# A decoder block's down projection as seven block products in eight parts, with three weight sums formed in DRAM

## Chip, cores, metric

One core of a Trainium2 chip runs the whole program. The metric is the device time of one execution in microseconds. Three runs of the kernel before gave 2439.49, 2440.13 and 2441.36 us; their median is 2440.13. A change of under 0.2% (4.9 us) is treated as no change.

## The reference, cut to what matters

`x` has 512 tokens of 2048 channels; everything is float32.

```python
def _sq_relu_mlp(h, w_up, w_down):
    return jnp.square(jax.nn.relu(h @ w_up)) @ w_down

h = x
for l in range(DEPTH):                       # DEPTH = 1
    a = _rmsnorm(h, norm1_w[l])
    h = h + _token_mix(a, w_in[l], ...)      # four head groups and an output projection
    m = _rmsnorm(h, norm2_w[l])
    h = h + _sq_relu_mlp(m, w_ffn_up[l], w_ffn_down[l])
return _rmsnorm(h, final_norm_w)
```

The change concerns the last product: the hidden activations, 512 x 8192, times `w_ffn_down`, 8192 x 2048, added to `h`, and the final norm. What is computed stays the same up to rounding.

## The kernel before, in words

**Float32 products as three matmuls.** Each float32 operand is split into a high part `hi`, which is a cast to the matmul's type (ScalarE), and a low part `lo`, the operand minus `hi` (VectorE). A product is then hi x hi + hi x lo + lo x hi, three matmuls into one accumulation in PSUM. So each weight tile of 128 x 1024 is loaded from DRAM by SP's queue into a `raw` tile, then cast (L296), then subtracted (L297). `ahead` keeps loads and splits some tiles in front of TensorE. The buffers `raw`, `hi` and `lo` rotate over three tiles in the mixers and over four later (`rotating`, `more_w`).

**Stages.** (1) The prologue normalises `x`. (2) The mixers: the input projection (`proj`, line 437, one block of 128 columns at a time, two weight halves each, 52 calls) is interleaved with the small products of the four head groups. (3) The output projection `wout` (lines 1218 to 1226). (4) The up phase (from about 1117 us of the profile). It already multiplies in blocks of two by two with seven products instead of eight: for each of 32 pairs `p` of hidden blocks, the products m = 1 to 7 (`units`) use sums of the four weight blocks that `prepare` forms on VectorE (line 1409) before the split (lines 1411 and 1412); the sums of the activations were prepared once. The products of the first four pairs with m = 1 and 2 are made early (`EARLY`) to fill a gap. `combine` (lines 1480 to 1498) puts the seven results together in a tile `ct`, applies ReLU and square on ScalarE into `rc`, and GpSimd stores `rc` (0.5 MB per pair) to DRAM tiles `hp[p]`. (5) The down phase: for 16 groups of four hidden blocks, SP loads the group's activations back from `hp` (they are split into `hd`) and eight weight tiles; for each 512 output columns `n` and each 128 tokens `t`, `down_tile` (lines 1544 to 1546) does 4 x 3 matmuls of 128 x 128 by 128 x 512 into the PSUM tile `dn`, and VectorE adds `dn` to the residual `h` (line 1547). In the last group the final norm follows each row `t`: squares on ScalarE, a multiplication with the norm weights `fw` on VectorE (line 1571), the power on GpSimd (line 354), a scaling (lines 1579 and 1581), and a store (line 1582). The residual tiles wait in DRAM (`hr`) during the up phase and are loaded by GpSimd at line 1534.

**What sets the order.** The program's text gives each instruction a priority. A planner then fixes each engine's queue ahead of time: it walks through a modelled execution and gives an engine, whenever it is free, the instruction of highest priority whose operands and memory are ready. Between `in_order(EN.PE)` and the next `in_order` the queue of TensorE alone follows the text word for word; at the very start (until `lora_proj`) SP, ScalarE and VectorE do too. The queues themselves run in order: an instruction that waits holds up what stands behind it.

Of the kernel before, what the change touches and what calls it, by code (L numbers as in the profile page):

```python
# [10 lines left out]
F32 = mybir.dt.float32  # L11
# [180 lines left out]
def tile_trunk(ctx: ExitStack, tc: tile.TileContext, ins, out):  # L192
# [44 lines left out]

    EARLY = 4
    hp = [pd.tile([128, 1024], F32, tag=f"h1_{p}", name=f"h1_{p}") for p in range(32)]
# [3 lines left out]
    seq += [(ins["wup"][2 * p, q], 1024) for p in range(EARLY) for q in range(2)]  # L243
    down0 = len(seq)
    hidden = {}

    def hidden_of(g):
        for q in range(2):
            hidden[len(seq)] = (g, q)
            seq.append((hp[2 * g + q], 1024))  # L250

    hidden_of(0)
    for g in range(16):
        for n in range(4):
            if n == 2 and g < 15:
                hidden_of(g + 1)
            seq += [(ins["wdn"][2 * g + q, n], 1024) for q in range(2)]
    raws, halves = {}, {}
    st = {"l": 0, "s": 0, "n": 0, "cap": down0}
    hd = {}  # L260

    def halves_of(i, w):
        if 2 <= i < 4:
            return S("wh", F32R), S("wl", F32R)
        if i in hidden:
            g, q = hidden[i]
            if q == 0:
                hd[g] = [(AT if g == 0 else HD)("hd").rearrange("p a t -> p (a t)") for _ in range(2)]
            return [x[:, 1024 * q:1024 * q + 1024] for x in hd[g]]
        if i >= len(seq) - 8:  # L270
            both = AT("wd").rearrange("p a t -> p (a t)")
            return both[:, :1024], both[:, 1024:]
        return new_halves()

    more_w, turn_of = [], {}

    def rotating(tag, dt):

        turn_of[tag] = turn_of.get(tag, -1) + 1 if more_w else -1
        if more_w and turn_of[tag] % 4 == 3:  # L280
            return more_w[0].tile([128, 1024], dt, tag=tag, name=tag)
        return pw.tile([128, 1024], dt, tag=tag, name=tag, bufs=3)
# [7 lines left out]
    def ahead(more=0, by=V, splits=True):  # L290

        while True:
            if splits and st["s"] < min(st["l"], st["n"] + 2 + more):
                r, w = raws.pop(st["s"])
                h, l = halves_of(st["s"], w)
                A.copy(h[:, :w], r[:, :w])  # L296
                by.tensor_tensor(l[:, :w], r[:, :w], h[:, :w].bitcast(F32), op=ALU.subtract)  # L297
                halves[st["s"]] = (h, l)
                st["s"] += 1
            elif st["l"] < min(st["cap"], st["n"] + 4 + more):  # L300
# [124 lines left out]
    def proj():  # L425
        w = len(BLOCKS[blk[0]])
        blk[0] += 1
        acc = pp.tile([128, 512], F32, tag="pp", name="acc")
        n = 0
        for q in range(2):  # L430
            h, l = weights()
            for k in range(8):
                kk = 8 * q + k
                wh, wl = h[:, w * k:w * k + w], l[:, w * k:w * k + w]
                rh, rl = ahi[kk // 4][:, kk % 4], alo[kk // 4][:, kk % 4]
                for a, b in ((wh, rh), (wh, rl), (wl, rh)):
                    PE.matmul(acc[:w], a, b, start=n == 0, stop=n == 47)  # L437
# [803 lines left out]
    more_w.append(ctx.enter_context(tc.tile_pool(name="w4", bufs=1, reuse_waits="tile")))  # L1241
# [151 lines left out]
    units = [(p, m) for p in range(32) for m in (((1,) if p >= EARLY else ()) + (5, 6, 7, 3) + ((2,) if p >= EARLY else ()) + (4,))]  # L1393
    rw, uh, bank = {}, {}, {}

    def load_pair(p):
        for b, (f, q) in (("11", (0, 0)), ("12", (1, 0)), ("22", (1, 1)), ("21", (0, 1))):
            rw[p, b] = new_raw() if (p == 0) or b == "21" else RW("raw2")
            nc.sync.dma_start(rw[p, b], ins["wup"][2 * p + f, q])
# [50 lines left out]
    for j in range(2 * EARLY):  # L1450
# [11 lines left out]
        else:  # L1462
# [5 lines left out]
            G.dma_start(hp[p][:, 256:512], c11)  # L1468
# [3 lines left out]
    def combine(p, m, acc):  # L1472

        if p not in cts:
            cts[p] = pu.tile([128, 6, 256], F32, tag="ct", name="ct", bufs=2)
            if p < EARLY:
                A.copy(cts[p][:, 2], X[p])
        ct = cts[p]
        if m == 1:
            A.copy(ct[:, 2], acc)  # L1480
        elif m == 5:
            A.copy(ct[:, 5], acc)
        elif m == 6:
            V.tensor_tensor(ct[:, 0], ct[:, 2], acc, op=ALU.add)
        elif m == 7:
            V.tensor_tensor(ct[:, 1], ct[:, 0], acc, op=ALU.add)
            V.tensor_tensor(ct[:, 3:5], bc(ct[:, 5:6], (128, 2, 256)), ct[:, 0:2], op=ALU.subtract)
        elif m == 3:
            V.tensor_tensor(ct[:, 3], ct[:, 3], acc, op=ALU.add)
        elif m == 2:  # L1490
            V.tensor_tensor(ct[:, 2], ct[:, 2], acc, op=ALU.add)
        else:
            V.tensor_tensor(ct[:, 1], ct[:, 1], acc, op=ALU.add)
            rc = pu.tile([128, 4, 256], F32, tag="rc", name="rc", bufs=2)
            for w in [slice(0, 1), slice(2, 4)] if p < EARLY else [slice(0, 4)]:
                A.activation(rc[:, w], ct[:, w.start + 1:w.stop + 1], AF.Relu)
                A.activation(rc[:, w], rc[:, w], AF.Square)
                G.dma_start(hp[p].rearrange("p (b t) -> p b t", b=4)[:, w], rc[:, w])

    for u, (p, m) in enumerate(units):  # L1500
# [13 lines left out]
        if u + 3 >= len(units):  # L1514
            st["cap"] = len(seq)
            ahead(u + 3 - len(units))
# [6 lines left out]

    in_order()
# [3 lines left out]
    S = lambda n="s", dt=F32: pg.tile([128, 512], dt, tag="s", name=n, bufs=14)  # L1528
    small = lambda n, w: pg.tile([128, w], F32, tag=f"q{w}", name=n, bufs=6)
    HD = lambda n: pg.tile([128, 4, 512], F32R, tag="hd", name=n, bufs=4)  # L1530
    ht = [[pg.tile([128, 512], F32, tag="h", name=f"h{t}_{n}", bufs=16) for n in range(4)] for t in range(4)]
    for n in range(4):
        for t in range(4):
            G.dma_start(ht[t][n], hr[t][n])
    AT_OF = {(0, 0): 1, (0, 1): 0, (1, 0): 2, (1, 1): 3}

    def down_tile(hs, w, t, n):
        acc = BK("dn")
        for k in range(4):
            h, l = w[k // 2]  # L1540
            ws = slice(512 * (k % 2), 512 * (k % 2) + 512)
            at = 1024 * (k // 2) + 256 * AT_OF[k % 2, t // 2] + 128 * (t % 2)
            hh, hl = (x[:, at:at + 128] for x in hs)
            PE.matmul(acc, hh, h[:, ws], start=k == 0, stop=False)  # L1544
            PE.matmul(acc, hh, l[:, ws], start=False, stop=False)  # L1545
            PE.matmul(acc, hl, h[:, ws], start=False, stop=k == 3)  # L1546
        V.tensor_tensor(ht[t][n], ht[t][n], acc, op=ALU.add)  # L1547

    for g in range(15):
        if g == 0:  # L1550
            weights(2), weights(2)
        for n in range(4):
            if n == 2:
                weights(), weights()
            more = 2 * n if g == 14 else 0
            w = [weights(more), weights(more)]
            for t in range(4):
                down_tile(hd[g], w, t, n)


    frow = [S(f"fw{i}") for i in range(4)]
    for i in range(4):
        nc.scalar.dma_start(frow[i], ins["norms"][2:3, 512 * i:512 * i + 512].broadcast_to([128, 512]))
    wl = [weights() for _ in range(8)]
    for t in range(4):
        ss, s1 = small("ss", 4), small("s1", 2)
        y = [S("y") for _ in range(4)]
        for n in range(4):
            down_tile(hd[15], wl[2 * n:2 * n + 2], t, n)
            squares(ss, ht[t][n], n)  # L1570
            V.tensor_tensor(y[n], ht[t][n], frow[n], op=ALU.mult)
            if n == 2:
                V.tensor_reduce(s1[:, 0:1], ss[:, 0:3], axis=AX.X, op=ALU.add)
                V.tensor_scalar(s1[:, 0:1], s1[:, 0:1], 1.0 / D, EPS, op0=ALU.mult, op1=ALU.add)
        V.tensor_scalar(s1[:, 0:1], ss[:, 3:4], 1.0 / D, s1[:, 0:1], op0=ALU.mult, op1=ALU.add)
        rsqrt(s1[:, 1:2], s1[:, 0:1], 1)
        for i in range(4):
            if i % 2:
                A.activation(y[i], y[i], AF.Copy, scale=s1[:, 1:2])
            else:  # L1580
                V.tensor_scalar(y[i], y[i], s1[:, 1:2], None, op0=ALU.mult)
            (nc.sync, nc.scalar)[i % 2].dma_start(out[0, 128 * t:128 * t + 128, 512 * i:512 * i + 512], y[i])
# [17 lines left out]
```

## Time and profile before

| | us |
|---|---|
| median of three runs | 2440.13 |
| the profiled execution, its own time | 2442.88 |
| its span, first to last instruction | 2441.1 |
| TensorE matmuls busy | 2399.6 |
| VectorE busy | 1549.2 |
| ScalarE busy | 849.9 |
| first down matmul | 1735.1 |
| bytes moved by DMA | 290.44 MB, 119 GB/s on average |

A row of the windows gives, for one stretch of the span, its length, the busy time of each engine with its number of instructions, the granted clock of TensorE (1.00 is full), the mean busy share of the 16 DMA engines and the rate that they moved. A row of a group gives line, engine, operation, output and inputs, shapes, count, then busy time, mean nanoseconds, and the idle time of the engine before these instructions with what ended it. In a tile's view the row has minimum, median and maximum duration in nanoseconds and the first and last start. A row of the timeline gives start and duration in us. PE is TensorE, PEld its weight load, DVE VectorE, ACT ScalarE, POOL GpSimd; SPq and ACTq are DMA issues of SP and ScalarE. Durations of neighbouring instructions of one engine overlap in part.

### The profile page before, as it was taken

The numbers are of one execution on the slowest core, as the hardware profiler recorded it, in microseconds if no ns is written. First come the engines' busy times: TensorE is split into PE (matmuls) and PEld (weight loads), VectorE is DVE, ScalarE is ACT, GpSimd is POOL, SyncE is SP. The second block draws the span as 40 slices with busy tenths as digits, with TensorE's granted clock in tenths as the row PEclk, the third lists the DMA queues.
The fourth block names the chain that finished last, engine by engine and source line by source line (L and its number), as shares of the span: only waits on it lengthen the run. The fifth ranks groups of instructions, "written<-read, shape, count | busy, mean of one in ns | idle before, by whom it ended". The sixth has DMA issues, their size and how long they took to land.

```text
span 2441.1 us, 36437 instructions
## 1 busy us (share of the span) xinstructions
PE 2399.6 (98%) x15074; PEld 2060.5 (84%) x15074; DVE 1549.2 (63%) x2523; ACT 849.9 (35%) x1168; POOL 76.8 (3%) x110
## 2 busy tenths in 40 slices
PE   7999999999999999999999999999999999999998
PEld 6777778778777888889999999999988888888886
DVE  5676855765684444678877777777655455554555
ACT  5223233223322232455544444444422222222232
POOL 1000000000000000010000000000100000000000
PEclk9999999999999999999999999999999999999999
DMA  5221212212221426655444444443543343433441
GB/s 185 75 77 44 79 46 77 86 62 70 78 82 54 137 89 230 209 192 172 134 136 136 135 132 135 133 132 111 216 133 118 112 138 105 135 116 110 138 137 70
DMA packets 86950, 290.44 MB, mean 119 GB/s; under 512 B 9984, under 2 KB 10496, under 8 KB 86784
## 3 DMA queue, kind: packets, MB, share of 16 engines
q1 hardware_dynamic: 75312, 255.53, 33.2%
q0 software_dynamic: 7296, 25.17, 2.6%
q10 hardware_dynamic: 4176, 7.41, 0.9%
q8 instruction: 118, 1.93, 0.3%
q14 instruction: 48, 0.39, 0.0%
HBM read 258.71 MB, written 29.36 MB: 118 GB/s over the span
## 4 chain that ended last, share of the span: by engine, by line
PE 89%; DVE 8%; issue 1%; POOL 1%; DMA 1%; ACT 0%; SPq 0%; POOLq 0%; DVEq 0%; ACTq 0%
PE acc L437 18%; PE dn L1546 9%; PE dn L1545 9%; PE dn L1544 9%; PE p L1418 8%; PE p L1419 8%; PE p L1420 8%; PE wo L1226 2%; PE wo L1218 2%; PE wo L1219 2%; DVE lo L297 1%; PE acc L460 1%; DVE xi L546 1%; DVE xm L547 1%; DVE XT L548 1%
## 5 line engine op out<-in xcount | busy, mean ns | idle before, releaser
L296 ACT CAST hi<-raw 128x1024 fp32r<-128x1024 f32 x282 | 296.3, 1051 | 887.6 <-PE dn L1546 464.8
L297 DVE TENSOR_TENSOR lo<-raw,hi 128x1024 fp32r<-128x1024 f32 x280 | 341.8, 1222 | 247.1 <-ACT hi L296 230.5
L1544 PE MATMUL dn<-hi,hd 128*128 128x512 f32 x960 | 373.4, 389 | 0.0
L1545 PE MATMUL dn<-lo,hd 128*128 128x512 f32 x960 | 373.4, 389 | 0.0
L1546 PE MATMUL dn<-hi,hd 128*128 128x512 f32 x960 | 373.4, 389 | 0.0
L437 PE MATMUL acc<-ah,hi 128*128 128x512 f32 x832 | 336.3, 404 | 0.0
L437 PE MATMUL acc<-al,hi 128*128 128x512 f32 x832 | 335.5, 403 | 0.0
L437 PE MATMUL acc<-ah,lo 128*128 128x512 f32 x832 | 333.7, 401 | 0.0
L1411 ACT CAST hi<-raw 128x1024 fp32r<-128x1024 f32 x216 | 223.9, 1050 | 301.9 <-DVE raw L1409 171.6
L1547 DVE TENSOR_TENSOR h<-h,dn 128x512 f32<-128x512 f32 x256 | 175.2, 685 | 222.5 <-PE dn L1546 214.2
L1412 DVE TENSOR_TENSOR lo<-raw,hi 128x1024 fp32r<-128x1024 f32 x216 | 261.5, 1222 | 63.9 <-ACT hi L1411 63.5
L1546 PEld LDWEIGHTS dn<-hi,hd 128*128 128x128 f32 x960 | 180.2, 188 | 37.4
L1544 PEld LDWEIGHTS dn<-hi,hd 128*128 128x128 f32 x960 | 180.2, 188 | 37.3
L1545 PEld LDWEIGHTS dn<-lo,hd 128*128 128x128 f32 x960 | 180.2, 188 | 37.3
L437 PEld LDWEIGHTS acc<-ah,hi 128*128 128x128 f32 x832 | 156.4, 188 | 38.4 <-issue 7.4
L437 PEld LDWEIGHTS acc<-ah,lo 128*128 128x128 f32 x832 | 156.4, 188 | 34.6 <-issue 2.9
L437 PEld LDWEIGHTS acc<-al,hi 128*128 128x128 f32 x832 | 156.4, 188 | 32.0 <-issue 1.9
L1409 DVE TENSOR_TENSOR raw<-raw,raw 128x1024 f32<-128x1024 f32 x124 | 151.3, 1220 | 5.0 <-DMA raw<-in_wup_dram 3.9
L1418 PE MATMUL p<-s2h,hi 128*128 128x256 f32 x256 | 72.4, 283 | 0.0
L1419 PE MATMUL p<-s2l,hi 128*128 128x256 f32 x256 | 72.4, 283 | 0.0
L1420 PE MATMUL p<-s2h,lo 128*128 128x256 f32 x256 | 72.4, 283 | 0.0
L1418 PE MATMUL p<-s1h,hi 128*128 128x256 f32 x256 | 72.4, 283 | 0.0
(487 smaller groups left out, 4583.1 us busy)
## 6 DMA issues: line engine op xcount, KB each, us to landing
raw<-in_wup_dram SPq DMA_DIRECT2D x136, 512.0 KB, 4.0
raw<-in_wdn_dram SPq DMA_DIRECT2D x128, 512.0 KB, 4.4
raw<-in_win_dram SPq DMA_DIRECT2D x106, 512.0 KB, 3.6
raw<-in_wout_dram SPq DMA_DIRECT2D x48, 512.0 KB, 3.7
raw<-h SPq DMA_DIRECT2D x32, 512.0 KB, 3.3
h<-rc POOLq DMA_DIRECT2D x28, 512.0 KB, 4.3
x<-in_x_dram SPq DMA_DIRECT2D x16, 256.0 KB, 6.5
h<-in_x_dram SPq DMA_DIRECT2D x16, 256.0 KB, 4.6
```

Source lines behind the costliest of these rows:

```text
L296: A.copy(h[:, :w], r[:, :w])
L297: by.tensor_tensor(l[:, :w], r[:, :w], h[:, :w].bitcast(F32), op=ALU.subtract)
L437: PE.matmul(acc[:w], a, b, start=n == 0, stop=n == 47)
L1411: A.copy(h, r)
L1412: V.tensor_tensor(l, r, h.bitcast(F32), op=ALU.subtract)
L1418: PE.matmul(acc, wh, rh[:, k], start=k == 0, stop=False)
L1419: PE.matmul(acc, wh, rl[:, k], start=False, stop=False)
L1420: PE.matmul(acc, wl, rh[:, k], start=False, stop=k == 7)
L1544: PE.matmul(acc, hh, h[:, ws], start=k == 0, stop=False)
L1545: PE.matmul(acc, hh, l[:, ws], start=False, stop=False)
L1546: PE.matmul(acc, hl, h[:, ws], start=False, stop=k == 3)
L1547: V.tensor_tensor(ht[t][n], ht[t][n], acc, op=ALU.add)
```

## The change

The down projection is cut into eight parts `c` of 1024 hidden rows. Within a part, tokens, hidden rows and output columns are each halved, and the two-by-two block product is done with seven products. Output columns come in two slices `s` of 512 columns of each half. One product (c, s, m) has two weight slabs `i` of 128 x 1024 and 24 matmuls (`down`). Its left operand, a sum of activation blocks, comes ready from DRAM: `combine` forms four sums more in the up phase and ScalarE's queue stores eight blocks (1 MB, in runs of 1 KB) per pair to `hq`. The right operand is a weight block for m = 1, 2, 3, and a sum of blocks for m = 4, 5, 6, 7. The sums for 5, 6 and 7 are formed in DRAM: `add_weights` copies one block to a fresh DRAM tile through SP's queue, and GpSimd issues an accumulating DMA that adds a second one, 96 copies and 96 accumulations of 0.5 MB in all. One step of it follows each `proj` and each fifth unit of the up phase in the text. The sum for m = 4 is made by VectorE from the `raw` tiles of products 2 and 6. The results for m = 1, 5, 6, 7 are kept in SBUF (`kept`) over the parts and combined in the last one; those for 2, 3, 4 go to the residual at once. The loop that writes up blocks pairs them differently (`hidden(p)`), and TensorE's order is now given by the text in the down phase too. `raw` has four tiles more there. Nothing changes in the mixers and the output projection but the steps of `add_weights`.

```diff
+    def hidden(p):
+        return 8 * (p // 4) + p % 4, 8 * (p // 4) + 4 + p % 4
-    hp = [pd.tile([128, 1024], F32, ...) for p in range(32)]
+    hq = [pd.tile([128, 8, 4, 256], F32, ...) for c in range(8)]
+    e11 = [pd.tile([128, 256], F32, ...) for p in range(EARLY)]
...
+    def wd(c, i, j, s, q):
+        return ins["wdn"][4 * c + 2 * i + q, 2 * j + s]
+    sums = {}
+    def add_weights():
+        late = None
+        for c in range(8):
+            for s in range(2):
+                for q in range(2):
+                    b11, b12, b22 = (wd(c, i, j, s, q) for i, j in ((0, 0), (0, 1), (1, 1)))
+                    for m, x, y in ((5, b12, b11), (7, b12, b22), (6, b22, None)):
+                        d = sums[m, c, s, q] = pd.tile([128, 1024], F32, tag=f"t{m}{c}{s}{q}", name="t")
+                        nc.sync.dma_start(d, x)
+                        if late:
+                            G.dma_start(*late, accum_op=ALU.add, max_dma_last_dim=1024)
+                        late = d, sums[5, c, s, q] if y is None else y
+                        yield
+        G.dma_start(*late, accum_op=ALU.add, max_dma_last_dim=1024)
+    adding = add_weights()
...
         ahead()
+        next(adding, None)                       # at the end of proj
...
-    units = ... (((1,) if p >= EARLY else ()) + (5, 6, 7, 3) + ((2,) if p >= EARLY else ()) + (4,))
+    units = ... (((1, 2) if p >= EARLY else ()) + (5, 6, 7, 3, 4))
...
+    DPROD = {1: 2, 2: 1, 3: 0, 4: 4, 5: 6, 6: 7, 7: 5}
+    DORD = [(1, 5, 7, 6, 2, 4, 3)] * 7 + [(1, 5, 6, 2, 3, 7, 4)]
+    def down_ahead(i):
+        while ds["s"] < len(dseq):
+            e = dseq[ds["s"]]
+            if e[0] == "w" and dslab[e[1:]] > i + 3:
+                break
...
+            if e[0] == "w" and e[3] == 4:
+                _, c, s, _, q = e
+                r, other = dr["w", c, s, 2, q], dr["w", c, s, 6, q]
+                V.tensor_tensor(r[1], r[1], other[1], op=ALU.add)
...
+            A.copy(h, r[1])
+            V.tensor_tensor(l, r[1], h.bitcast(F32), op=ALU.subtract)
...
+        while ds["l"] < ds["s"] + 5 and down_load():
+            pass
...
     def combine(p, m, acc):                      # its last step, m == 4
             V.tensor_tensor(ct[:, 3], ct[:, 3], acc, op=ALU.add)
+            A.activation(ct[:, 3], ct[:, 3], AF.Relu)
+            A.activation(ct[:, 3], ct[:, 3], AF.Square)
+            V.tensor_tensor(ct[:, 5:7], ct[:, 2:4], ct[:, 3:5], op=ALU.subtract)
+            V.tensor_tensor(ct[:, 7], ct[:, 6], ct[:, 2], op=ALU.subtract)
+            V.tensor_tensor(ct[:, 0], ct[:, 1], ct[:, 7], op=ALU.add)
+            nc.scalar.dma_start(hq[p // 4][:, :, p % 4], ct)
...
+        if u % 5 == 4:
+            next(adding, None)
...
+    homes["raw"].append((pg, 4))
+    def down(c, s, m, i, accs):
+        down_ahead(dslab[c, s, m, i])
+        h, l = dh.pop((c, s, m, i))
+        hi, lo = dop[c, m]
+        for t in range(2):
+            for k in range(2):
+                kk = 2 * i + k
...
+                PE.matmul(accs[t], xh, h[:, ws], start=kk == 0, stop=False)
+                PE.matmul(accs[t], xh, l[:, ws], start=False, stop=False)
+                PE.matmul(accs[t], xl, h[:, ws], start=False, stop=kk == 3)
...
+    for c in range(7):
+        for s in range(2):
+            for m in DORD[c]:
+                accs = [BK("dn") for _ in range(2)]
+                for i in range(2):
+                    down(c, s, m, i, accs)
+                for t in range(2):
+                    if m in (2, 3, 4):
+                        x = ht[t + 2 * (m == 4)][s + 2 * (m == 3)]
+                    else:
+                        x = kept[m, s, t]
+                    if c == 0 and m in (1, 5, 6, 7):
+                        A.copy(x, accs[t])
+                    else:
+                        add(x, accs[t])
```

Part 7 follows with the same matmuls; there each result is combined into the residual tiles (for m = 7, four additions and subtractions for each `t`), and each finished tile is squared on ScalarE and multiplied by `fw`. Rows 0 and 1 are scaled and stored after its product 3, rows 2 and 3 after its product 4, the last one.

More of the change, by code (lines that the diff above doesn't have):

```diff
@@ L242, in tile_trunk @@
     seq += 2 * [(ins["wout"][n, q], 1024) for n in range(4) for q in (4, 5, 2, 3)]
[L243 to L257, printed above, removed]
+    seq += [(ins["wup"][hidden(p)[0], q], 1024) for p in range(EARLY) for q in range(2)]
     raws, halves = {}, {}
-    st = {"l": 0, "s": 0, "n": 0, "cap": down0}
-    hd = {}
+    st = {"l": 0, "s": 0, "n": 0}
     def halves_of(i, w):
@@ L264, in halves_of @@
             return S("wh", F32R), S("wl", F32R)
[L265 to L272, printed above, removed]
         return new_halves()
-    more_w, turn_of = [], {}
+    homes = {"hi": [(pw, 3)], "lo": [(pw, 3)], "raw": [(pw, 3)]}
+    at = {t: -1 for t in homes}
     def rotating(tag, dt):
[L279 to L282, printed above, removed]
+        at[tag] = i = (at[tag] + 1) % sum(n for _, n in homes[tag])
+        for p, n in homes[tag]:
+            if i < n:
+                return p.tile([128, 1024], dt, tag=tag, name=tag, bufs=n)
+            i -= n
     def new_halves():
@@ new lines, in tile_trunk, with down_load @@
+    ds = {"l": 0, "s": 0, "w": 0}
+    ring = []
+    def down_load():
+        if ds["l"] >= len(dseq):
+            return False
+        e = dseq[ds["l"]]
+        if e[0] == "w" and e[3] == 4:
+            ds["l"] += 1
+            return True
+        n = sum(n for _, n in homes["raw"])
+        if len(ring) >= n and ring[-n][0] > 0:
+            return False
+        if e[0] == "x":
+            src, uses = hq[e[1]][:, DPROD[e[2]]].rearrange("p k t -> p (k t)"), 1
+        else:
+            _, c, s, m, i = e
+            src = sums[m, c, s, i] if m in (5, 6, 7) else wd(c, m != 1, m == 3, s, i)
+            uses = 2 if m in (2, 6) else 1
+        r = new_raw()
+        nc.sync.dma_start(r, src)
+        dr[e] = [uses, r]
+        ring.append(dr[e])
+        ds["l"] += 1
+        return True
@@ L1521, in tile_trunk @@
             combine(*post.pop(0))
-    in_order()
+    while next(adding, adding) is not adding:
+        pass
+    in_order(EN.PE)
     mid.close()
@@ new lines, in tile_trunk, with finish, write @@
+    for i in range(4):
+        nc.gpsimd.dma_start(frow[i], ins["norms"][2:3, 512 * i:512 * i + 512].broadcast_to([128, 512]))
+    fss = [small("fss", 4) for _ in range(4)]
+    def finish(t, n):
+        squares(fss[t], ht[t][n], n)
+        V.tensor_tensor(ht[t][n], ht[t][n], frow[n], op=ALU.mult)
+    def write(t):
+        s1 = small("s1", 2)
+        V.tensor_reduce(s1[:, 0:1], fss[t], axis=AX.X, op=ALU.add)
+        V.tensor_scalar(s1[:, 0:1], s1[:, 0:1], 1.0 / D, EPS, op0=ALU.mult, op1=ALU.add)
```

162 lines of the change are left out of this document (99 added, 63 removed).

## Prediction

> **What bounds the kernel now.** I read the page's totals first, then busy time by stage (the windows), then the down products' tile.
>
> ```profile
> span 2441.1 us, 36437 instructions
> PE 2399.6 (98%) x15074; PEld 2060.5 (84%) x15074; DVE 1549.2 (63%) x2523; ACT 849.9 (35%) x1168; POOL 76.8 (3%) x110
> ```
> ```profile
> core 0: us, PE busy (x) PEld busy (x) DVE busy (x) ACT busy (x) POOL busy (x), PEclk, DMA share, GB/s
> 70.00:900.00 830.00, 824.25 (x5454) 642.66 (x5453) 525.83 (x1296) 244.48 (x410) 24.98 (x18) 1.00 0.24 74
> 900.00:1117.00 217.00, 209.08 (x1041) 176.93 (x1040) 134.92 (x170) 90.30 (x132) 13.67 (x24) 0.98 0.59 192
> 1117.00:1735.00 618.00, 618.00 (x5191) 618.00 (x5190) 483.01 (x534) 302.65 (x356) 19.27 (x36) 1.00 0.42 138
> 1735.00:1800.00 65.00, 65.00 (x290) 53.87 (x289) 33.19 (x39) 18.40 (x18) 9.11 (x17) 1.00 0.62 218
> 1800.00:2387.00 587.00, 587.00 (x2592) 486.21 (x2591) 305.01 (x356) 143.62 (x140) 0.00 (x0) 1.00 0.39 122
> 2431.60:2441.10 9.50, 0.00 (x0) 0.00 (x0) 2.48 (x5) 2.06 (x4) 0.55 (x1) 0.64 0.29 111
> ```
> ```profile
> L1544 PE MATMUL dn<-hi,hd x960: 389/389/395, 1735.1 to 2387.2; 128*128 128x512 f32 x192
> L1546 PE MATMUL dn<-wd,hd x64: 388/389/389, 2388.3 to 2431.2; 128*128 128x512 f32 x64
> ```
> The rows are, in order, mixers, output projection, up phase, the start of the down phase, its body, and the tail. TensorE has no idle time from 1117 to 2431.6 at a granted clock of 1.00; VectorE is at 52% in the body of the down phase (305.01 of 587), ScalarE at 24%. So a matmul taken out there is time taken out, until another engine or the DMA gets full.
>
> **Products removed.** Before: 16 groups x 4 x 4 output tiles x 12 = 3072 matmuls, from 1735.1 to 2431.2 + 0.4 = 2431.6, that is 696.5 us, or 226.7 ns each (the 389 in the row is latency, since neighbours overlap). After: 8 parts x 2 halves x 7 products x 24 = 2688 of the same form. 384 fewer x 0.2267 = **-87.1 us**. The Trainium skill (TensorE: Matmul & The Clock Gate, Back-to-back issue gap) gives about 131 ns per 512-column matmul in a sustained stream; by it the gain would be only 50 us, an estimate from that page. The trace does not agree with it here: it shows 226.7.
>
> **Work added to VectorE and ScalarE in the down phase.**
> ```profile
> 1823.20 0.68 DVE L1547 TENSOR_TENSOR h<-h,dn 128x512 f32<-128x512 f32 x1
> 1823.79 1.22 DVE L297 TENSOR_TENSOR hd<-raw,hd 128x1024 fp32r<-128x1024 f32 x1
> 1824.93 1.22 DVE L297 TENSOR_TENSOR lo<-raw,hi 128x1024 fp32r<-128x1024 f32 x1
> 1826.06 0.68 DVE L1547 TENSOR_TENSOR h<-h,dn 128x512 f32<-128x512 f32 x1
> 1826.66 1.22 DVE L297 TENSOR_TENSOR hd<-raw,hd 128x1024 fp32r<-128x1024 f32 x1
> ```
> ```profile
> L297 DVE TENSOR_TENSOR lo<-raw,hi 128x1024 fp32r<-128x1024 f32 x280 | 341.8, 1222 | 247.1 <-ACT hi L296 230.5 <-PE wo L1226 16.6
> L296 ACT CAST hi<-raw 128x1024 fp32r<-128x1024 f32 x282 | 296.3, 1051 | 887.6 <-PE dn L1546 464.8 <-PE acc L437 299.2 <-PE wo L1219 79.9
> ```
> Back to back, a split's subtraction takes 1.14 us (1823.79 to 1824.93) and an addition 0.60 (1826.06 to 1826.66), less than their durations. The tightest stretch is the second half (s=1) of a part: 14 weight slabs, 6 operands of the next part and 2 sums for product 4 make 22 x 1.14 = 25.1, and 14 additions x 0.60 = 8.4: 33.5 us against 168 matmuls x 0.2267 = 38.1. Even by durations (1.22 and 0.68) it is 36.4. ScalarE has 20 casts x 1.05 = 21, and in part 0 it also takes 16 of the 28 additions as copies. Splits run three slabs (8.2 us) ahead, so I take **0** in parts 0 to 6. If the casts do not overlap, it costs what the second rival below says.
>
> Part 7 is different. 33 splits and sums x 1.14 = 37.6; 76 additions and multiplications x 0.60 = 45.6; four row ends of about 1.3 = 5: 88 us against 76.2 of TensorE. Three slabs (3.4) are done ahead, the last two additions of part 6 (1.2) are owed: VectorE would end 9.8 us after TensorE.
> ```profile
> 2433.97 0.88 DVE L1581 TENSOR_SCALAR y<-y,s 128x512 f32<-128x512 f32 x2 [0.66 <-POOL s L354]
> 2434.72 0.95 ACTq L1582 DMA_DIRECT2D out_dram<-y  x2
> ```
> From the last scaling (2434.8) to the end (2441.1) are 6.3 us, so the tail becomes at most 16 instead of 9.5 (+6.5); at least it grows by a second row's scaling and the overhang of product 7 (10 x 0.60 = 6.0 against a product's 5.4), about +1.5. I take **+5**.
>
> **Start of the down phase.** The first half-part loads 7 operands and 12 slabs of 0.524 MB, and 16 residual tiles of 0.262 MB: 14.2 MB in 38.1 us, 372 GB/s. The first 65 us of this phase moved 218 GB/s at a DMA share of 0.62, which would be 352 at a full share: 40 us, 2 late. At 218 itself it is 65 us, 27 late, but the residual tiles are first needed at the fifth product: the 10 MB of the others then take 46, 8 late, less what was loaded ahead. **+4**, bounds 0 and 27. Later a part loads 24 slabs and 7 operands, 16.2 MB in 336 x 0.2267 = 76.2 us: 213 GB/s, below 218 at 0.62.
>
> **Up phase.**
> ```profile
> 1459.57 1.23 DVE L1412 TENSOR_TENSOR lo<-raw,hi 128x1024 fp32r<-128x1024 f32 x1 [0.64 <-ACT hi L1411]
> 1467.02 0.69 DVE L1487 TENSOR_TENSOR ct<-ct 128x512 f32<-128x512 f32 x1
> 1467.63 1.22 DVE L1412 TENSOR_TENSOR lo<-raw,hi 128x1024 fp32r<-128x1024 f32 x1
> 1470.03 0.41 DVE L1489 TENSOR_TENSOR ct<-ct,p 128x256 f32<-128x256 f32 x1
> 1470.36 1.22 DVE L1409 TENSOR_TENSOR raw<-raw,raw 128x1024 f32<-128x1024 f32 x1
> ```
> Per pair of blocks (seven products of 2.86 us, 20.0) VectorE gets one subtraction of 512 columns (0.61, 1467.02 to 1467.63) and two operations of 256 (0.33 each): 1.3 us more, on 78% busy by durations (483.01 of 618): hidden, and if it were not, 30 x 1.3 = 39. ScalarE takes over the store from GpSimd: its issues above cost 0.48 each, and it waits there for VectorE's last three operations, with the next casts queued behind; units are prepared three ahead (8.6 us), so hidden too. The other moves are small and have one answer: product 2 goes second with the same work, SP loads four saved tiles of 0.13 MB, and the loads of `fw` go from ScalarE to GpSimd, where nothing waits before the last part. DMA per pair: 2.1 MB of weights, a store of 1.05 MB (in runs of 1 KB) instead of 0.52, and 1.4 copies and 1.4 accumulations, 1.5 MB: 4.6 MB in 20.0 us = 231 GB/s, against 192 at a share of 0.59 in the output projection. Fits at equal efficiency (0.7); if an accumulation counts double, 268 GB/s, still under 329. **+2**, bounds 0 and, with 218 GB/s as the ceiling and double counting (5.35 MB, 24.5 us), 4.5 x 30 pairs = 136.
>
> **Mixers.** 52 copies and 52 accumulations, 1.05 MB per projection block of 16 us (830 / 52): 66 GB/s beside 74, below the 192 of the next stage.
> ```profile
> L1498 POOL DMA_DIRECT2D h<-rc x36 | 19.3, 535 | 597.0 <-ACT ct L1480 526.9 <-ACT rc L1497 70.0 <-ACT ct L1477 0.2
> ```
> GpSimd pays 0.54 us per issue, and its powers (`rsqrt`) queue behind an accumulation that still waits for its copy; that copy was issued a block earlier, so I take **+1**, if the order of the program holds.
>
> **Sum** against the profiled execution: 2441.1 - 87.1 + 5 + 4 + 2 + 1 = 2366 span, 2367.8 with the 1.8 us around it (2442.88 - 2441.1). That execution lies 2.75 above the median 2440.13, so **2365**. A gain beyond 87 has no source, as no other stage loses work: floor 2352 with some slack for the unknowns.
>
> **Rivals.** *First, the copies leave their place (slower).* They read inputs and write fresh DRAM, so nothing but the planner's order holds them back. What it does with such loads is in the trace:
> ```profile
> L1571 DVE TENSOR_TENSOR y<-h,fw x16: 691/692/693, 2391.5 to 2432.3; 128x512 f32<-128x512 f32 x16
> L1563 ACTq DMA_DIRECT2D fw<-in_norms_dram x4: 334/394/467, 1737.3 to 1746.5; - x4
> ```
> The loads of `fw` stand behind fifteen groups in the program and were issued 650 us before their use, as soon as their memory was free. The copies' memory is free from the start, and SP is the queue of the weight loads.
> ```profile
> 1739.17 3.74 POOL L1534 DMA_DIRECT2D h<-hr  x7
> 1746.59 0.54 POOL L1534 DMA_DIRECT2D h<-hr  x1 [0.32 <-DMA h<-hr]
> ```
> ```profile
> 298.99 1.04 ACT L296 CAST hi<-raw 128x1024 fp32r<-128x1024 f32 x1 [2.85 <-PE acc L437]
> 404.75 1.04 ACT L296 CAST hi<-raw 128x1024 fp32r<-128x1024 f32 x1 [3.11 <-PE acc L437]
> ```
> A queue ran about eight transfers ahead before it waited for a landing. In the mixers 12 weight halves take 105.8 us, 8.8 each, with two loads under way. If each round of two loads has eight copies and eight accumulations before it, a round moves 9.4 MB; at 333 GB/s (218 / 0.62 is 352, 122 / 0.39 is 313) that is 28.3 us where 17.6 are needed: 12 rounds x 10.7 = 129, hence **2494**. At 218 GB/s a round is 43.3, 308 late (2673); with the accumulations lagging, 5.2 MB take 15.7, nothing late (2365). I take the middle, as it rests on the rates per share of two stages. It turns the sign where a round exceeds 17.6 + 75 / 12 = 23.9 us, below 395 GB/s, more than any full share above. Against it: the planner may keep other bounds than memory, and the trace has no copy that shows it. The Trainium skill (DMA: Bandwidth & Descriptors, Issuing engines are not separate DMA queues) says that transfers of SP, ScalarE and GpSimd share the same 16 engines; by that, accumulations are no traffic beside the loads but among them. No run here shows a DRAM-to-DRAM rate yet.
>
> *Second, VectorE becomes the bound.* If each of the 14 slabs of a half also waits 0.65 for its own cast (the 0.64 above), s=1 needs 33.5 + 9.1 = 42.6 against 38.1: 8 x 4.5 = 36 late, **2401**. Against it: in the rows above splits follow each other without such a wait.
>
> *Third, DMA fills up in the up phase.* At 218 GB/s as the ceiling and without double counting a pair takes 21.2 us, 36 late (2401); with it 136, **2501**. It turns the sign at 20.0 + 75 / 30 = 22.5 us. Against it: the shares above leave room.
>
> *Fourth, little comes of it:* half of the first case (75 late), about **2440**.
>
> **Chances.** Forecast 0.58 (2365, itself between 2354 and 2390), VectorE-bound 0.11, DMA-bound up phase 0.04, nothing 0.04, copies ahead 0.23. A change under 0.2% (4.9 us) is about what measurement cannot tell from none. Faster 0.69, same 0.04, slower 0.27. The range from 2352 to 2475 leaves out most of the case of copies ahead, about 0.2.
>
> **What would show it.** Right: `dn` matmuls 2688, 609 us from first to last, no idle TensorE there; the mixers' stage still 830 us, copies spread to 1735. Wrong: SP issuing dozens of copies before 400 us, TensorE or ScalarE waiting for `raw` in the mixers (first rival); casts or additions ending TensorE's waits after 1735 (second); `raw` from the up weights doing so before it (third).

## The result and the profile after

The changed kernel takes 2638.16 us (median of four runs, 2635.73 to 2641.52) against 2440.65 before: a ratio of 1.0811, interval 1.0792 to 1.0829. It is slower by 197.5 us where 75 less was forecast, and lies outside the range.

The page of the kernel after, from its first two parts (totals, and the span in 40 slices of 66 us):

```profile
span 2639.7 us, 36752 instructions
PE 2330.1 (88%) x14690; PEld 2000.5 (76%) x14690; DVE 1737.4 (66%) x2751; ACT 1007.1 (38%) x1416; POOL 159.8 (6%) x174
...
PE   4950670599999999999989999999997999999997
...
PEclk9975885699999999999999999999998999999998
DMA  9999999812221222346656444445438667666653
```

TensorE does 69.5 us less work than before (2399.6 to 2330.1; 87.1 were forecast), but its share of the span falls from 98% to 88%. The holes are in the first eight slices, some 1500 us ahead of the first of the new down products, and there the DMA engines are full. The windows by stage (prologue; mixers in two parts; output projection; up phase; start, body and last part of the down phase; tail):

```profile
0.00:70.00 70.00, 36.61 (x238) 34.33 (x239) 29.29 (x48) 27.77 (x64) 18.24 (x22) 0.95 1.05 298
70.00:500.00 430.00, 199.25 (x1285) 151.94 (x1284) 127.42 (x340) 56.49 (x97) 90.82 (x87) 0.72 1.05 237
500.00:1156.40 656.40, 651.57 (x4254) 511.93 (x4253) 406.95 (x984) 193.53 (x324) 22.16 (x16) 1.00 0.25 78
1156.40:1373.50 217.10, 209.00 (x1046) 176.90 (x1045) 135.34 (x171) 90.78 (x133) 13.66 (x24) 0.98 0.59 192
1373.50:1991.50 618.00, 618.00 (x5188) 618.00 (x5187) 516.40 (x626) 329.26 (x467) 5.77 (x11) 1.00 0.50 166
1991.50:2056.00 64.50, 49.42 (x206) 39.92 (x205) 34.69 (x35) 30.16 (x36) 5.46 (x11) 0.87 0.83 298
2056.00:2552.00 496.00, 496.00 (x2190) 410.82 (x2190) 409.60 (x435) 240.83 (x237) 0.00 (x0) 1.00 0.66 215
2552.00:2629.00 77.00, 70.23 (x297) 56.63 (x295) 73.49 (x103) 34.86 (x56) 2.08 (x2) 0.96 0.33 110
2629.00:2639.70 10.70, 0.00 (x0) 0.00 (x0) 4.18 (x11) 3.39 (x6) 1.56 (x2) 0.63 0.51 197
```

The first two of these stretches in the kernel before:

```profile
0.00:70.00 70.00, 51.73 (x322) 46.27 (x323) 39.10 (x77) 33.56 (x74) 7.57 (x12) 1.00 0.53 174
70.00:500.00 430.00, 426.48 (x2923) 330.95 (x2921) 295.02 (x774) 127.95 (x214) 13.46 (x8) 1.00 0.23 69
```

Read against the stages of before: the up phase starts at 1373.5 where it started at 1117 (256 later); it takes 618.0 as before; the down phase takes 637.5 where it took 696.5 (59 less); the tail 10.7 instead of 9.5. Together 256 - 59 + 1 = 198. The whole loss lies ahead of the up phase: nearly all of it in the first 500 us, the prologue and the first part of the mixers, where TensorE is busy 242 us less than before (15 and 227).

What did TensorE wait for? The waits of the kernel after, longest first (engine, tile and line, what it waited for, us in total, times, longest):

```profile
PE bk L680 <- DVE XT L672: 116.9, 1, 116.9
PE zb L941 <- DVE Sn L962: 109.7, 1, 109.7
PE bk L391 <- DVE x L380: 31.9, 5, 15.3
PE dn L1644 <- ACT m L1663: 14.3, 1, 14.3
```

Two single waits make 226.6 of the 256 us. Neither names a DMA or a weight tile. VectorE, which they name, was itself waiting. Its timeline at the end of the first gap and of the second:

```profile
274.13 0.18 DVE L853 TENSOR_SCALAR rk<-rk 128x4 f32<-128x4 f32 x1 [122.73 <-POOL rk L852]
...
487.26 0.69 DVE L763 TENSOR_TENSOR Y<-Y,rs 128x512 f32<-128x512 f32 x1 [115.13 <-POOL rs L362]
```

So VectorE stood 122.73 and 115.13 us for a power on GpSimd. And GpSimd's timeline shows where that power stood:

```profile
252.06 1.01 POOL L310 DMA_DIRECT2D t<-t  x1 [7.39 <-DMA t<-in_wdn_dram]
252.69 2.47 POOL L310 DMA_DIRECT2D t<-in_wdn_dram  x2
262.49 1.01 POOL L310 DMA_DIRECT2D t<-t  x1 [7.33 <-DMA t<-in_wdn_dram]
263.11 2.47 POOL L310 DMA_DIRECT2D t<-in_wdn_dram  x2
271.99 1.03 POOL L310 DMA_DIRECT2D t<-t  x1 [6.41 <-DMA t<-in_wdn_dram]
272.64 1.45 POOL L852 TENSOR_TENSOR rk<-ek,phalf 128x4 f32<-128x4 f32 x1
```

The power on 128 x 4 numbers takes 1.45 us. In GpSimd's queue it stands behind a long column of accumulations. Each group of three takes about 10 us: two accumulations are issued, then the third, the sum for product 6, has to wait 6 to 7 us until the sum for product 5, which it adds, has landed. GpSimd is busy only 6% of the span, but it stands in these waits, and the queue runs in order. At the end of the second gap it looks the same:

```profile
483.48 1.01 POOL L310 DMA_DIRECT2D t<-t  x1 [6.91 <-DMA t<-in_wdn_dram]
484.10 1.43 POOL L310 DMA_DIRECT2D t<-in_wdn_dram  x1
484.75 2.48 POOL L362 TENSOR_TENSOR rs<-va,mhalf 128x8 f32<-128x8 f32 x1
```

The tile's view tells when copies (SPq) and accumulations (POOL) were issued, and GpSimd's waits how long it stood:

```profile
L308 SPq DMA_DIRECT2D t<-in_wdn_dram x96: 488/587/2440, 2.6 to 374.1; - x96
...
L310 POOL DMA_DIRECT2D t<-in_wdn_dram x64: 1020/1450/1994, 11.4 to 494.2; - x64
```
```profile
POOL t L310 <- DMA t<-in_wdn_dram: 384.3, 34, 38.2
```

Of these 384.3 us, the views of the two lines put 295.6 down to accumulations and 88.6 to copies that had not landed. All 96 copies left before 375 us and the last accumulation at 503.1, though the program's text spreads them to the end of the up phase. The planner moved them to the front, as the first rival had it; but what they held up is the queue of GpSimd, and that rival had named the queue of the weight loads.

### The profile page after: what moved, and what is told of

Its sections match the earlier page's. It is cut to its first block, busy times and chain, and to the rows that moved or that the text cites. A ratio compares the mean times of both kernels' runs of the same rounds, so it can differ in the third digit from the quotient of the medians.

```text
span 2639.7 us, 36752 instructions
## 1 busy us (share of the span) xinstructions
PE 2330.1 (88%) x14690; PEld 2000.5 (76%) x14690; DVE 1737.4 (66%) x2751; ACT 1007.1 (38%) x1416; POOL 159.8 (6%) x174
## 3 DMA queue, kind: packets, MB, share of 16 engines
q0 software_dynamic: 53760, 60.30, 13.9%
## 4 chain that ended last, share of the span: by engine, by line
PE 69%; issue 15%; DVE 7%; POOL 4%; DMA 3%; ACT 1%; SPq 0%; POOLq 0%; DVEq 0%; ACTq 0%
PE acc L445 13%; PE p L1429 8%; PE p L1430 8%; PE p L1431 8%; PE dn L1645 7%; PE dn L1646 7%; PE dn L1644 7%; POOL t L310 3%; DMA t<-in_wdn_dram 2%; PE wo L1228 2%; PE wo L1227 2%; PE wo L1235 2%; DVE lo L281 1%; DMA h<-ct 1%; DVE xi L555 1%
## 5 line engine op out<-in xcount | busy, mean ns | idle before, releaser
L1644 PE MATMUL dn<-hi,x 128*128 128x512 f32 x896 | 351.1, 392 | 19.6 <-ACT m L1663 14.3
L1645 PE MATMUL dn<-lo,x 128*128 128x512 f32 x896 | 350.9, 392 | 2.2 <-DVE lo L1547 2.2
L1646 PE MATMUL dn<-hi,x 128*128 128x512 f32 x896 | 350.4, 391 | 0.0
L1546 ACT CAST hi<-raw 128x1024 fp32r<-128x1024 f32 x224 | 235.3, 1055 | 285.7 <-PE dn L1646 236.2
L1547 DVE TENSOR_TENSOR lo<-raw,hi 128x1024 fp32r<-128x1024 f32 x224 | 272.6, 1222 | 98.5 <-ACT hi L1546 97.1
L280 ACT CAST hi<-raw 128x1024 fp32r<-128x1024 f32 x162 | 169.7, 1049 | 417.0 <-PE acc L445 293.8
L1422 ACT CAST hi<-raw 128x1024 fp32r<-128x1024 f32 x216 | 226.4, 1050 | 215.0 <-PE p L1430 143.4
L1423 DVE TENSOR_TENSOR lo<-raw,hi 128x1024 fp32r<-128x1024 f32 x216 | 262.5, 1220 | 67.2 <-ACT hi L1422 66.6
L281 DVE TENSOR_TENSOR lo<-raw,hi 128x1024 fp32r<-128x1024 f32 x160 | 195.1, 1222 | 140.9 <-ACT hi L280 124.5
L1644 PEld LDWEIGHTS dn<-hi,x 128*128 128x128 f32 x896 | 169.4, 189 | 56.0 <-ACT m L1663 14.7
L1645 PEld LDWEIGHTS dn<-lo,x 128*128 128x128 f32 x896 | 169.4, 189 | 38.6 <-DVE lo L1547 3.5
L1646 PEld LDWEIGHTS dn<-hi,x 128*128 128x128 f32 x896 | 169.3, 189 | 35.1
L680 PE MATMUL bk<-con,XT 64*64 64x64 f32 x128 | 5.4, 245 | 116.9 <-DVE XT L672 116.9
L941 PE MATMUL zb<-Sn,KQ 128*128 128x128 f32 x24 | 5.0, 290 | 109.7 <-DVE Sn L962 109.7
L680 PEld LDWEIGHTS bk<-con,XT 64*64 64x64 f32 x128 | 4.8, 156 | 118.3 <-issue 117.3
```

Source lines behind the costliest of these rows:

```text
L1422: A.copy(h, r)
L1423: V.tensor_tensor(l, r, h.bitcast(F32), op=ALU.subtract)
L1546: A.copy(h, r[1])
L1547: V.tensor_tensor(l, r[1], h.bitcast(F32), op=ALU.subtract)
L1644: PE.matmul(accs[t], xh, h[:, ws], start=kk == 0, stop=False)
L1645: PE.matmul(accs[t], xh, l[:, ws], start=False, stop=False)
```

## Experiments

**The theory:** the accumulations, moved ahead, hold the mixers' powers in GpSimd's queue. **The rivals:** the traffic of copies and accumulations starves the weight loads (the mechanism on which the prediction's first rival was priced); or the sums cost their time wherever they stand.

**1. Copies and accumulations held in their places.**

```diff
-                        nc.sync.dma_start(d, x)
+                        tc.keep_in_program_order(nc.sync.dma_start(d, x))
-                            G.dma_start(*late, accum_op=ALU.add, max_dma_last_dim=1024)
+                            tc.keep_in_program_order(G.dma_start(*late, accum_op=ALU.add, max_dma_last_dim=1024))
```

> The 96 copies and the 96 accumulations stay where the program has them (one copy and one accumulation per projection block and per five units of the up phase). Theory (GpSimd's queue: the mixers' powers, L852 and L362, stand behind accumulations that the planner moved to the front): the two gaps of TensorE of 116.9 and 109.7 us go, and so do some 30 us of the first stage; the up phase starts within 10 us of 1117.5 again, and the time is 2639 - 256 = 2383 (2375 to 2395), faster than before by over 2%. Rival (traffic: copies and accumulations and weight loads want more than the DMA engines move): the same traffic, 158 MB of copies and accumulations, is now spread over 1735 us and not packed in 500, so the mixers recover too, but the up phase, with 231 to 268 GB/s wanted, gets late by up to 36 us: 2400 to 2420. Rival (the sums cost their time wherever they stand): no gain over the change, 2600 to 2640.

Measured: 2388.27 us (2384.92 to 2393.65), ratio to before 0.9788 [0.9771, 0.9805]. The waits at L680 and L941 are gone (1.5 us and none), and the up phase starts at 1120.2. The change of order alone is worth 250 us. The rival by which sums cost the same anywhere falls. Copies and accumulations are 100.7 MB by the DMA queues shown in the last section, not the 158 of the expectation. (The profiled execution of this experiment took 2393.65 us, 5.4 above its median; that matters where the profiles of later experiments are compared with it.)

**2. Only the accumulations held; the copies may run ahead.**

```diff
-                            G.dma_start(*late, accum_op=ALU.add, max_dma_last_dim=1024)
+                            tc.keep_in_program_order(G.dma_start(*late, accum_op=ALU.add, max_dma_last_dim=1024))
```

> Only the accumulations keep their place; the copies may still go to the front of SyncE's queue. Theory: the powers no longer stand behind accumulations, the two gaps are gone, and what is left of the loss is what the copies do to the first 70 us (x loads behind copies) and to weight loads, 15 to 50 us: 2395 to 2435. Rival (weight loads starve behind the copies, as the first rival of the prediction had it): the copies are 52 MB of the 105 that were in the way, so half or more of the 256 us stays: 2510 to 2600.

Measured: 2403.46 us (one run). All copies are issued between 2.6 and 239 us, so they did run ahead, and TensorE is busy 426.3 of the 430 us from 70 to 500. What is left over experiment 1 is not in the mixers: from 1117 to 1340 us TensorE is busy 212.75 of 223 us with the DMA engines at a share of 1.11 (222.98 at 0.86 in experiment 1). Both kernels have issued 51 accumulations before 1117 us. The other 45 go at the pace of the copies in experiment 1, the last at 1758.5 us. Here their copies are long there, and GpSimd issues them three per 15 us, the last at 1345.7: the order is held, not the time. In that stretch ScalarE stands 30.8 us until stores of `ct` have landed (6.3 in experiment 1), and TensorE 8.6 us for ScalarE's casts, so here a full DMA share goes with a loss of some 10 us.

**3. Copies free, no accumulations.**

```diff
-                        if late:
-                            G.dma_start(*late, accum_op=ALU.add, max_dma_last_dim=1024)
...
-        G.dma_start(*late, accum_op=ALU.add, max_dma_last_dim=1024)
```

> The copies stay free to move, and the accumulations are left out (products 5, 6 and 7 then multiply one weight block in place of a sum). Theory: as with the accumulations in their place, and a little better for their missing traffic: 2390 to 2430, no wait of TensorE over 30 us in the mixers. Rival (weight loads starve behind the copies): 96 copies still lie ahead of the weight loads, so 100 us or more of the 256 stay: 2480 or above.

Measured: 2384.29 us (one run). This is under the range of the theory, and only 0.3 above the next experiment, which has no copies: ninety-six copies ahead of the weight loads cost nothing that shows.

**4. No sums at all**, the floor.

```diff
-                        d = sums[m, c, s, q] = pd.tile([128, 1024], F32, tag=f"t{m}{c}{s}{q}", name="t")
-                        nc.sync.dma_start(d, x)
...
+                        sums[m, c, s, q] = x
```

> No copies and no accumulations at all (products 5, 6 and 7 read one plain weight block from the input in place of a sum, so the additions of weight blocks are left out). This is the floor for the sums: theory: 2370 to 2385, at most 10 us under the kernel with copies and accumulations in place, as their traffic fits beside the rest. Rival (the sums cost their time wherever they stand): 100 us or more under it. The start of the down phase (a wait for the memory of the last store, 11 us) and part 7 (8 us idle) stay as they are: down phase 637 us.

Measured: 2384.01 us (2382.07 to 2385.46), ratio 0.9766 [0.9750, 0.9782]. With their order kept, the sums in DRAM cost 2388.27 - 2384.01 = 4.3 us by the medians; that is under the 4.9 us that count as no change, and the two sets of runs overlap.

**5. Everything free, but the powers off GpSimd.** This separates queue from traffic: copies and accumulations leave their places as in the change, and only the powers go to VectorE.

```diff
-        G.tensor_tensor(dst, src, mhalf[:, :n], op=ALU.pow)
+        V.tensor_tensor(dst, src, mhalf[:, :n], op=ALU.mult)
-        G.tensor_tensor(rk, ek, phalf[:, :4], op=ALU.pow)
+        V.tensor_tensor(rk, ek, phalf[:, :4], op=ALU.mult)
```

> All copies and accumulations are free to move, as in the change; only the powers on GpSimd (L362, L852) are put on VectorE, as multiplications of the same size (the raising to -0.5 and 0.5 is left out). The traffic of copies and accumulations in the first 500 us is therefore the change's own. Theory (GpSimd's queue): the gaps of 116.9 and 109.7 us go, what is left is what the early copies cost the first stage: 2395 to 2430. Rival (the accumulations' traffic starves the loads, and the powers only show it): at least 150 of the 256 us stay, 2550 or more.

Measured: 2384.43 us (one run), again under the range of the theory. The windows and GpSimd's waits of this kernel:

```profile
0.00:70.00 70.00, 47.47 (x294) 42.42 (x295) 32.20 (x58) 32.20 (x71) 13.46 (x16) 0.98 1.03 323
70.00:500.00 430.00, 427.90 (x2846) 331.85 (x2844) 297.29 (x779) 129.72 (x217) 81.17 (x78) 1.00 1.09 263
```
```profile
POOL t L310 <- DMA t<-in_wdn_dram: 414.3, 34, 51.5
```

GpSimd stands in its waits even longer than in the change (414.3 us against 384.3), the DMA engines are even fuller (263 GB/s at a share of 1.09, against 237), and TensorE is busy 427.90 of 430 us. Same traffic, same queue, no loss in the mixers: what cost the 227 us there was the powers behind the accumulations, not the traffic. Even what the prologue loses through its own powers shrinks (47.47 busy of 70 us, where the change has 36.61 and the kernel before 51.73).

**6. The start of the down phase.** What is left over the forecast is in the down phase: 637.5 us for 2688 x 0.2267 = 609.4. Of these 28.1 us TensorE is idle for 21.9 (15.1 at the start, 6.8 in part 7), and its matmuls take 6.2 longer (busy 615.7). ScalarE's timeline of the kernel after, at its start:

```profile
2001.32 0.52 ACTq L1591 DMA_DIRECT2D h<-ct  x1
...
2021.64 2.05 ACT L1663 COPY m<-dn 128x512 f32<-128x512 f32 x4 [11.27 <-DMA h<-ct]
```

The first kept tile `m` lies where the last `ct` of the up phase lay. The store of that `ct`, issued at 2001.32, landed 20.3 us later (the median of these stores is 9.3), beside the loads of the down phase, and until then ScalarE could not copy the first product out of PSUM; its next casts stood behind that copy. Here the four `fw` tiles, needed only in part 7, were placed ahead of the kept tiles, onto the `ct`, on top of experiment 1.

```diff
+    frow = [pg.tile([128, 512], F32, tag="fw", name=f"fw{i}", bufs=4) for i in range(4)]
     kept = {(m, s, t): pg.tile([128, 512], F32, tag="m", name=f"m{m}", bufs=16)
             for s in range(2) for m in (1, 5, 6, 7) for t in range(2)}
-    frow = [pg.tile([128, 512], F32, tag="fw", name=f"fw{i}", bufs=4) for i in range(4)]
```

> Sums in place as in the first experiment, and the four rows of the last norm's weights are placed ahead of the kept product sums, so that they and not the first kept tiles lie where the last ct of the up phase lay. Theory (a wait for memory): the 14 us of TensorE behind ScalarE's first copy of a kept tile go, 2388 - 14 = 2374. Rival (the wait only hides the DMA rate, share 0.95 in the first 65 us of the down phase): another wait, for raw or for the residual tiles h, takes its place, and under 5 us come of it: 2384 or more.

Measured: 2381.75 us (2378.14 to 2384.41), ratio 0.9756 [0.9741, 0.9770]: 6.5 us under experiment 1, between theory and rival. The wait for `m` is gone, and one of 10.8 us takes its place (waits of this kernel):

```profile
PE dn L1644 <- ACT hi L1546: 16.1, 2, 10.8
```

Its end is ScalarE's cast of a weight slab whose load came late (a row of ScalarE's timeline):

```profile
1771.13 1.04 ACT L1546 CAST hi<-raw 128x1024 fp32r<-128x1024 f32 x1 [6.67 <-DMA raw<-in_wdn_dram]
```

From 1765 to 1802 us the DMA engines ran at a share of 1.00 and 376 GB/s, and TensorE had 29.31 of 37 us. So the wait for memory hid the DMA rate in part.

**7. Part 7 with twenty additions on GpSimd**, on top of experiment 1: those of products 1, 5 and 6 that touch SBUF alone.

```diff
+    gadd = lambda x, y: G.tensor_tensor(x, x, y, op=ALU.add)
+    gsub = lambda x, y: G.tensor_tensor(x, x, y, op=ALU.subtract)
...
-                    add(c12, x5)
-                    add(c22, x5)
+                    gadd(c12, x5)
+                    gadd(c22, x5)
```

> Sums in place as in the first experiment; in part 7, twenty additions and subtractions between SBUF tiles (those of products 1, 5 and 6) go from VectorE to GpSimd. Theory (VectorE bounds part 7): VectorE has 20 x 0.65 = 13 us less of its 74.5, TensorE's 8 us idle there shrink to 2 or less: 2388 - 6 = 2382 (2379 to 2384). Rival (the idle time is set by ScalarE's casts, or GpSimd's operations hinder VectorE's as they run beside them): within 2 us of 2388, or above.

Measured: 2388.85 us (2386.15 to 2391.80), no gain: the rival. The groups of VectorE from 2304 to 2372 us, here and then in experiment 1 (busy us, mean ns):

```profile
L1547 DVE TENSOR_TENSOR lo<-raw,hi 128x1024 fp32r<-128x1024 f32 x21 | 34.7, 1665 | 0.0
...
L1648 DVE TENSOR_TENSOR m<-m,dn 128x512 f32<-128x512 f32 x12 | 7.6, 675 | 0.0
```
```profile
L1547 DVE TENSOR_TENSOR lo<-raw,hi 128x1024 fp32r<-128x1024 f32 x22 | 26.4, 1218 | 0.7 <-ACT hi L1546 0.7
L1648 DVE TENSOR_TENSOR m<-m,dn 128x512 f32<-128x512 f32 x13 | 8.4, 679 | 0.0
```

While GpSimd adds, VectorE's subtraction of two SBUF tiles takes 1665 ns on average instead of 1218, and an addition that reads PSUM takes no longer (675 and 679). What was taken off VectorE came back as longer operations. In part 7 TensorE does wait less, 3.6 us instead of 6.8, but 17.5 us follow its last matmul instead of 10.8, with VectorE busy for 11.0 of them. The Trainium skill (SBUF — State Buffer, section "SBUF: two separate sides") says that a VectorE operation with two SBUF inputs and a GpSimd operation that reads SBUF hold one shared pair of ports in turn; this trace agrees.

**8. The three together**, with the sums done earlier:

```diff
-        if u % 5 == 4:
+        if u % 4 == 3:
             next(adding, None)
```

> The three together: sums in place and done 40 units before the up phase ends (every fourth unit in place of every fifth), kept tiles elsewhere, the twenty additions of part 7 on GpSimd. Theory: 2388 - 14 - 6 - 3 = 2365, 3.1% under the kernel before. Rival (the DMA rate at the start of the down phase): 2375 to 2382.

Measured: 2384.68 us (2381.28 to 2388.07), ratio 0.9769 [0.9754, 0.9783]. The down products end 626.3 us after they start (1737.5 to 2363.8) instead of 642.7 in the profile of experiment 1 (1738.3 to 2381.0), and 16.2 us follow (span 2380.0) where 10.8 did; VectorE is still busy for 9.7 us of them. As that execution of experiment 1 lies 5.4 us above its median, the medians show less of a gain: 3.6 us under experiment 1, within the spread of the runs. The forecast of 2365 failed by 20, and the rival's 2375 to 2382 lies below the median too.

**9. Ten residual tiles loaded later**, by SyncE between weight loads, and the sums done earlier, on top of experiment 6. `load_h` issues the loads of the listed tiles in program order, on SyncE unless GpSimd is named.

```diff
-            G.dma_start(ht[t][n], hr[t][n])
+    load_h([(t, n) for n, ts in ((0, range(4)), (2, range(2))) for t in ts], G)
...
+                if c == 0 and s == 0 and j == 5:
+                    load_h([(t, n) for n, ts in ((1, range(4)), (3, range(2))) for t in ts])
+                if c == 1 and s == 0 and j == 0:
+                    load_h([(t, n) for n in (2, 3) for t in (2, 3)])
```

> As the run with the kept tiles elsewhere, with every fourth unit in place of every fifth (sums done before the up phase ends), and of the 16 residual tiles only the six that the first half-part needs are loaded at once, the others by SyncE between the weight loads of the next parts: 2.6 MB and the last sums, some 2 MB, less in the first 40 us of the down phase. Theory (the DMA rate sets the start of the down phase: 14.2 MB and the sums at some 340 GB/s): TensorE's idle there falls from 11 us to 4 or less, 2382 - 7 = 2375 (2371 to 2378). Rival (the first slabs come late for the order of the loads, whatever else is moved): within 2 us of 2382.

Measured: 2381.70 us (2380.23 to 2382.50): no gain in time. From 1737 to 1802 us TensorE is busy 58.93 us of 65, where experiment 6 had 53.76, so the idle time there does halve, from 11.2 to 6.1, with the DMA share down from 0.99 to 0.86; so the DMA rate is part of it. Experiment 8, with the sums done earlier but all residual tiles loaded at once, has 57.59 there, so most of it seems to come from the earlier sums. The down products start at 1739.9 here and at 1736.8 there, which takes back 3.1 us, and why is not shown: over all kernels with the sums in place that start lies between these two.

**10. The kept sums merged in parts 5 and 6**, on top of experiment 9, so that part 7 adds each result straight to the residual tiles (for product 5, and in the same way for 1, 6 and 7):

```diff
-                    add(x5, accs[t])
-                    add(c12, x5)
-                    add(c22, x5)
+                    add(c12, accs[t])
+                    add(c22, accs[t])
```

> As the run before this one, and the kept sums are merged into the output tiles in parts 5 and 6, so that in part 7 each product goes straight to the tiles it feeds: 16 additions (9.6 us at 0.60) fewer on VectorE in part 7, 24 more in part 5's two halves and up to 24 more in part 6's, where VectorE had 82% of its time taken. Theory (VectorE alone bounds part 7): 6 to 8 us under the run before, 2367 to 2370. Rival (the moved additions make parts 5 and 6 VectorE-bound: 16 x 0.60 = 9.7 us against 10.3 free in a first half, 6.0 against 4.6 in a second half): it comes out even, 2373 to 2378.

Measured: 2380.36 us (2377.12 to 2381.23), ratio to before 0.9747 [0.9734, 0.9761]: the fastest median, though not separable from experiments 6 and 9. The windows of body and part 7, experiment 9 and then this one:

```profile
1802.00:2304.00 502.00, 502.00 (x2216) 415.83 (x2215) 417.24 (x447) 240.55 (x235) 0.00 (x0) 1.00 0.65 214
2304.00:2366.00 62.00, 55.25 (x236) 44.59 (x235) 60.34 (x87) 29.39 (x49) 2.01 (x2) 0.95 0.38 128
```
```profile
1802.00:2304.00 502.00, 496.29 (x2179) 409.69 (x2178) 436.40 (x486) 240.58 (x238) 0.00 (x0) 1.00 0.65 213
2304.00:2366.00 62.00, 62.00 (x276) 51.32 (x275) 59.61 (x82) 32.76 (x52) 1.12 (x2) 1.00 0.37 124
```

TensorE's 6.8 us of idle time in part 7 are gone, which shows that VectorE bounds that part. (In experiment 9 TensorE's waits there name ScalarE's cast, 5.3 us, and VectorE's subtraction, 1.5; ScalarE itself stands 16.4 us for VectorE there.) The additions now in parts 5 and 6 cost 5.7 us of TensorE there. The gain was given back, as the rival said; the times of both theory and rival were too low, as they were reckoned from the 2375 that experiment 9 did not reach.

## Why the prediction was wrong, point by point

**The step that failed is the one on the mixers:** "that copy was issued a block earlier, so I take **+1**, if the order of the program holds". The order did not hold, and the term was +256 us. The sentence before it named the right mechanism, that powers queue behind an accumulation that still waits. It was priced only for accumulations in their places. The 256 are two waits of 116.9 and 109.7 us, 13.8 more behind the powers of the prologue (L391: 31.9 against 18.1 before), and longer matmuls: TensorE's busy time up to the up phase is 11.4 us higher (1096.4 against 1085.1) for the same 6817 matmuls, with a granted clock of 0.72 from 70 to 500 us. The few us that remain are small waits.

**The chances failed with it.** The first rival had 0.23. Its evidence, the loads of `fw` issued 650 us ahead of their use, showed what the planner does with an instruction whose operands and memory are ready, and the copies read an input and write fresh memory. Nothing in the trace spoke against it except that no copy was in it. The rival deserved more than 0.23.

**The rival's price rested on a wrong mechanism.** It let weight loads stand behind eight copies and eight accumulations per round. Of the copies there were indeed about seven per round of 17.6 us (96 by 239 us in experiment 5), yet weight loads were not late there. The accumulations lagged, since each third waits for a landing: in experiment 5 the last of the 96 is issued at 537 us, about three per round. Its 263 GB/s are 4.6 MB per round, near the bound "5.2 MB take 15.7, nothing late". The Trainium skill (DMA: Bandwidth & Descriptors, Issuing engines are not separate DMA queues), cited there, has the transfers of all queues share the 16 engines. Experiment 2 agrees: with accumulations at a DMA share of 1.11, ScalarE's stores held it up 30.8 us instead of 6.3. But in the mixers a share of 1.09 starved nobody, so it sets no price there. That 2638 falls between the rival's 2494 and its upper 2673 is chance.

**The terms of the down phase:**
- *Products removed, -87.1:* right. There are 2688 matmuls, and in the body TensorE is busy 496.00 of 496.00 us, at a clock of 1.00.
- *0 in parts 0 to 6 after the start:* right. VectorE is busy 409.60 of 496 us there, and TensorE has no wait.
- *Start of the phase, +4 with bounds 0 and 27:* mis-sized. TensorE was idle for 15.1 us of 64.5 and ran at a clock of 0.87. The step counted bytes and left out who owned the memory: the kept tile under the last `ct`. Experiment 6 took 6.5 us away. Of the rest, experiment 9 shows the DMA rate, which the step did name, to be a part.
- *Part 7 and tail, +5:* 6.8 us idle in part 7 and 1.2 in the tail, 8.0. The mechanism (VectorE) was right, as experiment 10 shows; the delay fell inside the part, not behind it.

**Up phase and sums in their places, +2 and +1:** 4.3 us (experiments 1 and 4), with the up phase starting at 1120.2 instead of 1117.5. Nothing here contradicts the 3, though 4.3 cannot be told from none.

With its order kept, the change gives 2388.27, a gain of 52 us where 75 was forecast: the difference is the start of the down phase and part 7, with the longer matmuls there: 28.1 us and 1.2 in the tail where 9 were forecast.

## What to carry to other kernels

Before pricing a new DMA, ask what holds it in its place; if its operands are ready from the start, a planner may issue all of them at once, and the place in the text proves nothing. Then ask which small operations share its queue: an engine that is busy 6% of the time can stop the kernel when it stands in waits and something short but needed stands behind. And a full DMA share need not be a loss (experiment 5) but can be one (experiment 2); look at whose data comes late.

## What the runs showed of the hardware

The accumulating DMAs between DRAM tiles took 2.7 times the engine time of the copies. The DMA queues of the kernel after and of experiments 3 and 4 (packets, MB, share of 16 engines over the span):

```profile
q0 software_dynamic: 53760, 60.30, 13.9%
```
```profile
q1 hardware_dynamic: 91632, 352.54, 44.6%
...
q0 software_dynamic: 3072, 9.96, 1.1%
```
```profile
q1 hardware_dynamic: 88560, 302.20, 39.2%
```

Accumulations: 13.9% of 2639.7 us less 1.1% of 2382.5 is 340.7, or 3.5 us of all 16 engines for each of 96. Copies: 44.6% of 2382.5 less 39.2% of 2383.7 is 128.2, or 1.3 us each for the same 0.5 MB. In experiment 1, where they are spread out, it is 3.6 and 1.1 (queue shares of 15.5% and 43.6% of 2391.8 us, less 1.1% and 39.2% of 2383.7). The two also differ in their packets: an accumulation has 528 of about 1 KB, a copy 32 of 16 KB. How much of the price is the adding and how much the small packets is not shown. Issuing an accumulation of an input block took GpSimd 1.0 to 2.0 us (median 1.45; 1.0 in experiment 1), where the prediction had 0.54 from the loads of `h`.

Two more points were not expected: the granted clock of TensorE was 0.72 over the 430 us in which it idled half the time, and the same matmuls took 11.4 us longer, so idle time cost a little more than itself (after the wait of 10.8 us of experiment 6 too, the next matmuls show 0.80 and 0.63 us where the usual duration is 0.39); and VectorE's subtraction of two SBUF tiles took on average over a third longer in the stretch with GpSimd's additions (experiment 7).
